# An encoder layer on one core: the second tile's scale as a dot on TensorE, in the place of products of zeros, and the square of x's last tile on VectorE

## The chip, the core and the metric

The kernel runs on one core of one Trainium2 chip. The metric is the time of the slowest core of one execution in device microseconds, here that of the only core, as the median of several runs. The core's engines are TensorE (matrix products; PE in the profile, with its weight loads as PEld), VectorE (DVE), ScalarE (ACT), GpSimd (POOL) and SyncE (SP), which here mostly issues the loads. The engines run apart from each other and wait for each other by semaphores; each works through its own row of instructions in order.

## The reference, cut to what matters

One layer of an encoder, 1024 positions of 1024 channels, in float32. A condition vector c gives six vectors of 1024 values, of which the first two scale and shift the normalised input:

```python
mod = jax.nn.silu(c) @ w_ada + b_ada
sh1, sc1, gt1, sh2, sc2, gt2 = jnp.split(mod[:, None, :], N_MOD, axis=-1)

h = rmsnorm(x, norm1_g) * (1.0 + sc1) + sh1
z = h @ w_in
u, v, q, k, va, gate_a, gate_b = jnp.split(z, cuts, axis=-1)
...
x = x + gt1 * (merged @ w_o)
h2 = rmsnorm(x, norm2_g) * (1.0 + sc2) + sh2
f_gate, f_up = jnp.split(h2 @ w_ffn_in, 2, axis=-1)
x = x + gt2 * ((jax.nn.silu(f_gate) * f_up) @ w_ffn_out)
```

`rmsnorm` divides each position by the root of the mean square of its 1024 channels. The scale of one tile of 128 channels is 128 dots of length 1024: silu(c) with 128 columns of `w_ada`.

## The kernel before, in words

The activations lie transposed: channels on the 128 partitions, positions along the row. The 1024 channels are 8 tiles (`KT`), and the positions are worked on in two halves of 512. `half(0)` opens the program. It loads x in tiles, and for each tile squares it (ScalarE or VectorE), adds two squares at a time (VectorE), and lets TensorE sum them over the partitions into `total`. From the sums come root and reciprocal (`root`, `rcol`), which TensorE spreads over the partitions into the bank `rp`.

Scale and shift of a tile are two columns of `mod`. `ada_dot` makes one column: VectorE multiplies 128 rows of `w_ada` (one output channel on each partition, 1024 weights along the row) by `silu_c`, silu(c) spread over all partitions, and accumulates along the row in one SCALAR_TENSOR_TENSOR of 128x1024; ScalarE then adds bias and gain and writes the column of `mod`. `ada_pair(k)` loads the two sets of rows for tile k: scale and shift. The sets of tiles 0 and 1 (`r`, `r1`) are loaded at the start, the first with `w_q` and `w_kv` between their halves.

Then a loop runs over the tiles k. In it VectorE makes `x = x * mod[scale] * root`, ScalarE makes the high part `hH` (a cast of x + shift to the short float32 that TensorE multiplies fast), VectorE the low part `hL`; the weights of q and k are split in the same way into `wh` (ScalarE) and `wl` (VectorE). TensorE multiplies high by high, low by high and high by low into the banks of `qps` and `kps`. In the loop's turn k the two dots for tile k+1 are made, the scale's dot ahead of `hL` of tile k and the shift's dot behind it. The halo, 128 positions of the other half, is normalised in turns 4 and 7 (`halo_four`).

While TensorE has nothing to do in the start-up it multiplies zeros into banks that will later be summed into: `open_bank` is one product of 128x512 that opens a bank, and `keep_going` adds more, in the numbers of `ZEROS = (9, 2, 7)`. The last seven stand between the spread of the root and the first real products.

All loads are issued by SyncE in the order of the program. Instructions inside `half(0)`'s start-up and loop keep the order in which the code writes them on each engine. All waits are set by the framework from the tiles that are read and written. `small`, `mid`, `wpool` and `psum` are pools with a fixed number of buffers; `at_bank` takes the next of four banks of PSUM.

The rows of `w_ada` for a scale were laid out on the host in `_layout`, as `w_ada1`: 8 pairs of 128 x 2048.

Of the kernel before, what the change touches and what calls it, by code (L numbers as in the profile page):

```python
# [8 lines left out]
F32 = mybir.dt.float32  # L9
F32R = mybir.dt.float32r  # L10
BF16 = mybir.dt.bfloat16
AF = mybir.ActivationFunctionType
ALU = mybir.AluOpType
# [3 lines left out]
P = 128  # L17
D = 1024
S = 1024
KT = D // P  # L20
# [16 lines left out]
ZEROS = (9, 2, 7)  # L37
# [4 lines left out]
def kernel(  # L42
# [43 lines left out]
    V, A, G, T = (Engine(e) for e in (nc.vector, nc.scalar, nc.gpsimd, nc.tensor))  # L86
# [3 lines left out]
    const = ctx.enter_context(pool("const"))  # L90
# [17 lines left out]
    def at_bank():  # L108
        return psum.tile([P, 512], F32, tag="at", name=nm("at"))
# [7 lines left out]
    def midt(dt, shape):  # L117
        return mid.tile([P, 2048], dt, tag="mid", name=nm("mid")).rearrange(
            "p (a b) -> p a b", a=shape
        )  # L120
# [9 lines left out]
    def load(dst, src):  # L130
        tc.keep_in_program_order(nc.sync.dma_start(dst, src))  # L131
# [40 lines left out]
    zeros = const.tile([P, P], F32R, tag="zeros", name="zeros")  # L172
    V.tensor_scalar(zeros, ones, 0.0, None, op0=ALU.mult)
    V.memset(crow, 0.0)
    identr = const.tile([P, P], F32R, tag="identr", name="identr")
# [3 lines left out]
    epsc = const.tile([P, 1], F32, tag="epsc", name="epsc")  # L179
    V.memset(epsc, EPS)  # L180

    cc = const.tile([P, 72], F32, tag="cc", name="cc")
    bada, g1c, g2c, bsT = cc[:, :48], cc[:, 48:56], cc[:, 56:64], cc[:, 64:72]
    base = const.tile([P, 48], F32, tag="base", name="base")

    def load_cond():
# [9 lines left out]
    def silu_cond(pcs, i0=0):  # L196
        for i, pc in enumerate(pcs, i0):
            A.activation(silu_c[:, i * 512 : (i + 1) * 512], pc, AF.Silu)

    mod = const.tile([P, 48], F32, tag="mod", name="mod")  # L200
    acc_mod = const.tile([P, 48], F32, tag="acc_mod", name="acc_mod")
    SH1, SC1, GT1, SH2, SC2, GT2 = (8 * i for i in range(6))
# [5 lines left out]
                                   in1=g, op0=ALU.add, op1=ALU.mult)  # L208
        V.tensor_scalar(base[:, GT1:SH2], bada[:, GT1:SH2], 0.5, None, op0=ALU.mult)

    def ada_dot(r, col, cast=None, then=None):

        c1 = slice(col, col + 1)
        V.scalar_tensor_tensor(
            out=r, in0=r, scalar=1.0, in1=silu_c, op0=ALU.mult, op1=ALU.mult,
            accum_out=acc_mod[:, c1],
        )
        if then is not None:
            then()
        if cast is not None:  # L220
            A.copy(*cast)
        factor, added = 1.0, bada
        if GT1 <= col < SH2:
            factor, added = 0.5, base
        for sc, g in ((SC1, g1c), (SC2, g2c)):
            if sc <= col < sc + 8:
                factor, added = g[:, col - sc : col - sc + 1], base
        A.activation(mod[:, c1], acc_mod[:, c1], AF.Identity, bias=added[:, c1], scale=factor)

    def ada_pair(k):  # L230
        r = midt(F32, 2)
# [59 lines left out]
    def keep_going(bank, one, zero, n):  # L291

        for _ in range(n):
            T.matmul(bank, zero, one.unsqueeze(1).to_broadcast([P, 4, P]), start=False, stop=False)
# [272 lines left out]
    def half(hf):  # L567
# [4 lines left out]
        if hf == 0:  # L572
            in_order[0] = True
            xt2 = [midt(F32, 4) for _ in range(2)]
            xt = [xt2[k // 4][:, k % 4, :] for k in range(KT)]
            halo = midt(F32, 16)
            xh, qh = halo[:, :KT, :], halo[:, KT:, :]
            hl4 = midt(F32R, 16)

            for k, n in ((0, 2), (2, 2), (4, 2), (6, 1), (7, 1)):  # L580
                load(xt2[k // 4][:, k % 4 : k % 4 + n, :].rearrange("p a b -> p (a b)"),
                     xA[:, k * HALF : (k + n) * HALF])
                if k == 2:
                    load_cond()
            hd_store = lambda q, f: f(
                hd[0, q * HALF : (q + 1) * HALF, :].rearrange("(a p) t -> p a t", p=P), xt2[q])
            load(cc, cols)
            r = ada_pair(0)
            wq0, wk0 = (wpool.tile([P, UNIT], F32, tag="raw", name=nm("raw")) for _ in range(2))
            r1 = midt(F32, 2)  # L590
            load(wq0[:, :512], w_q[0][:, :512])
            load(r1[:, 0, :], w_ada1[1, :, :D])
            load(wk0[:, :512], w_kv[0][:, :512])
            load(r1[:, 1, :], w_ada1[1, :, D:])
            load(wq0[:, 512:], w_q[0][:, 512:])
            base_bias = bias_base()
            A.activation(sm(QPK, "es"), ones[:, :QPK], AF.Silu)
            build_bias(*base_bias, range(BIAS))

            total = at_bank()  # L600
            open_bank(total, zeros, zeros)
            keep_going(total, zeros, zeros, ZEROS[0])
            cond = silu_rows()
            sqs = [midt(F32, 4) for _ in range(2)]
            sq = [sqs[k // 4][:, k % 4, :] for k in range(KT)]
            add = lambda i, j: V.tensor_tensor(sq[i], sq[i], sq[j], op=ALU.add)
            square = lambda k: A.activation(sq[k], xt[k], AF.Square)

            def square_dve(k):
                V.tensor_tensor(sq[k], xt[k], xt[k], op=ALU.mult)  # L610

            def column_sums(q, last=False):

                for i in range(NT):
                    T.matmul(total[:, i * P : (i + 1) * P], q[:, i * P : (i + 1) * P], ones,
                             start=False, stop=last and i == NT - 1)

            square(0)
            square(1)
            add(0, 1)  # L620
            column_sums(sq[0])
            square(2)
            square_dve(3)
            add(2, 3)
            column_sums(sq[2])
            square_dve(5)
            square(4)
            silu_cond(cond[:1])
            add(4, 5)
            column_sums(sq[4])  # L630
            square(6)
            square(7)
            silu_cond(cond[1:], 1)
            add(6, 7)
            column_sums(sq[6], True)
            root = sm(5, "ms")
            A.activation(root[:, :NT], total.rearrange("p (a b) -> p a b", b=P)[:, :, 0], AF.Sqrt, scale=1.0 / D, bias=epsc)
            wq, wk = ([wpool.tile([P, UNIT], F32R, tag=x, name=nm(x)) for x in ("wh", "wl")]
                      for _ in range(2))
            ada_dot(r[:, 0, :], SC1, then=ada_base)  # L640
            V.reciprocal(rcol[0][:, :NT], root[:, :NT])
            A.copy(wq[0][:, :512], wq0[:, :512])
            ada_dot(r[:, 1, :], SH1)
            rp = at_bank()
            kbk = [at_bank() for _ in range(2)]
            open_bank(kbk[0], identr, zeros)
            keep_going(kbk[0], identr, zeros, ZEROS[1])
            for i in range(NT):
                T.matmul(rp[:, i * P : (i + 1) * P], rcol[0][:, i : i + 1].to_broadcast([P, P]), ident,
                         start=True, stop=True)  # L650
            open_bank(kbk[1], identr, zeros)
            keep_going(kbk[1], identr, zeros, ZEROS[2])
            hH = [hid(), hid()]
            hL = [hid(), hid()]
        else:
            hH, hL = h_next
            in_order[0] = True
# [4 lines left out]
        if hf == 1:  # L662
            kbk = [at_bank() for _ in range(3)]
            kps = [kbk[t][:, :256] for t in range(nkv)]
        for k in range(KT):
            if hf == 0:
# [24 lines left out]
                if k == 0:  # L691
                    rb = ss_tile()[:, :HALF]
                    A.copy(rb, rp)
                    tot4 = at_bank()
                    kbk.append(at_bank())
                    kps = [kbk[t // 2][:, (t % 2) * 256 : (t % 2 + 1) * 256] for t in range(nkv)]
                elif k == 2:
                    A.activation(qh, xh, AF.Square)
                elif k == 3:
                    A.activation(root[:, NT:], tot4[:, 0:1], AF.Sqrt, scale=1.0 / D, bias=epsc)  # L700
# [31 lines left out]
                    load(xh.rearrange("p a b -> p (a b)"), xA[:, KT * HALF :])  # L732
                cast = (w_next[0], raw) if src is not None else None
                if k < KT - 1:
                    ada_dot(r[:, 0, :], SC1 + k + 1, cast)
                if k == 3:
                    V.reciprocal(rcol[0][:, NT:], root[:, NT:])
                V.scalar_tensor_tensor(out=hL[k // 4][:, k % 4, :], in0=x, scalar=sh,
# [1185 lines left out]
def _layout(inputs):  # L1924
# [10 lines left out]
    def col(v):  # L1935
        return v.reshape(-1, 128).T
# [5 lines left out]
    w_b = a["w_b"][0].reshape(2, 4, 64, 1024).transpose(1, 0, 2, 3).reshape(512, 1024)  # L1942
    w_f = a["w_ffn_in"][0]
    ada = a["w_ada"][0].T.reshape(6, 8, 128, 1024)
    out = {
        "xA": np.concatenate([xt[:, t].reshape(8, 128, -1).transpose(1, 0, 2).reshape(128, -1)
                              for t in (slice(0, 512), slice(512, 640))], axis=1),
        "xB": xt[:, 512:],
        "c": a["c"][0],
        "cols": np.concatenate([col(a["b_ada"][0]), col(a["norm1_g"][0]), col(a["norm2_g"][0]),  # L1950
                                a["gm_b_s"][0].T], axis=1),
        "rowv": np.concatenate([a["gm_v_g"][0], a["q_norm_g"][0], a["k_norm_g"][0],
                                a["attn_sink"][0]]),
        "w_ada1": ada[[1, 0]].transpose(1, 2, 0, 3).reshape(8, 128, 2048),
        "w_ada2": ada[2:].reshape(32, 128, 1024),
        "w_u": tm(w_in[:, 0:512], 2),
        "w_v": tm(w_in[:, 512:1024], 2),
# [32 lines left out]
```

## Time and profile before

| | |
|---|---|
| median of 3 runs | 1226.87 us (1226.71 to 1227.76) |
| the profiled execution | 1226.14 us, its span 1224.2 us |
| TensorE busy | 1218.0 us of the span |
| VectorE busy | 898.1 us |
| ScalarE busy | 578.9 us |
| zeros in the last group ahead of the first real product | 8 products from 13.60 us on |
| first real product | 15.59 us |

The profile is of one execution on the chip. A busy TensorE is one that has an instruction in its pipe: multiplying zeros counts as busy. Rows of the timeline merge neighbouring instructions of the same kind, so a row's duration is that of the group. In names, `mid` is any tile of the pool of that name (x, its squares, the rows of `w_ada`), `at` and `mm` are banks of PSUM, `raw` are weights as loaded, `wh` and `wl` their high and low parts. Line 79 is the helper that all compute instructions go through, line 131 the one for loads, so rows are told apart by names and shapes. The 512 KB loads of `w_ada` are 128x1024.

### The profile page before, as it was taken

To read this page: it belongs to the slowest core of one execution; us is meant where nothing else is said; L and a number is where in the kernel's file an instruction comes from. 1 tells how busy PE (TensorE), PEld (TensorE's weight loads), DVE (VectorE), ACT (ScalarE), POOL (GpSimd) and SP (SyncE) were. 2 spreads that over 40 slices of the span, in tenths; PEclk is the share of its full clock that TensorE was granted. 3 is DMA by queue.
4 is the path that set the end of the run, shared out by engine and by line. 5 is a ranking of instruction groups with operands and counts; after the bars stand their busy time and mean duration, and the time that the engine had idled before them with its cause. 6 is when DMAs were issued, how large, how long until landed. Compare 5 with 4: busy or idle time off the path is not lost.

```text
span 1224.2 us, 15615 instructions
## 1 busy us (share of the span) xinstructions
PE 1218.0 (99%) x5693; PEld 1015.8 (83%) x5693; DVE 898.1 (73%) x1450; ACT 578.9 (47%) x944; POOL 148.7 (12%) x178
## 2 busy tenths in 40 slices
PE   9999999999999999999999999999999999999998
PEld 7888888888888888888888888888888888888887
DVE  8988877788878766878797766675676766765646
ACT  5667855367855443635453233333333334433341
POOL 0024323114331000001000001010000000010001
PEclk9999999999999999999999999999999999999999
DMA  9721169621076333597413446445555439995542
GB/s 364 283 87 52 35 235 357 233 86 52 36 273 225 120 105 121 195 317 277 149 52 120 172 155 224 167 174 209 189 189 189 168 150 364 393 368 190 189 172 103
DMA packets 75936, 230.77 MB, mean 189 GB/s; under 512 B 8658, under 2 KB 8914, under 8 KB 71124
## 3 DMA queue, kind: packets, MB, share of 16 engines
q1 hardware_dynamic: 61444, 161.62, 37.4%
q0 software_dynamic: 14416, 68.17, 14.9%
q8 instruction: 44, 0.72, 0.2%
q14 instruction: 32, 0.26, 0.1%
HBM read 174.70 MB, written 55.05 MB: 188 GB/s over the span
## 4 chain that ended last, share of the span: by engine, by line
PE 98%; DMA 0%; DVE 0%; ACT 0%; issue 0%; SPq 0%; DVEq 0%; ACTq 0%
PE mm L79 51%; PE at L79 47%; DMA mid<-in_xA_dram 0%; DVE mid L79 0%; ACT mid L79 0%; ACT wh L79 0%; ACT h L79 0%; DVE crow L79 0%; ACT mod L79 0%; DVE zeros L79 0%; DVE ones L79 0%; SPq L131 0%; DVE identr L79 0%; DVEq L79 0%; ACTq L79 0%
## 5 line engine op out<-in xcount | busy, mean ns | idle before, releaser
L79 PE MATMUL mm<-mid,wh 128*128 128x512 f32 x704 | 217.4, 390 | 0.0
L79 ACT CAST wh<-raw 128x1024 fp32r<-128x1024 f32 (+1 forms) x151 | 154.4, 1024 | 118.7 <-PE mm L79 44.3
L79 DVE TENSOR_TENSOR wl<-raw,wh 128x1024 fp32r<-128x1024 f32 (+1 forms) x137 | 161.5, 1183 | 64.4 <-ACT wh L79 63.9
L79 PEld LDWEIGHTS mm<-mid,wh 128*128 128x128 f32 x704 | 131.7, 188 | 27.1
L79 PE MATMUL mm<-mid,wl 128*128 128x512 f32 x352 | 137.0, 389 | 0.0
L79 PE MATMUL mm<-wh,h 128*128 128x512 f32 x384 | 125.0, 397 | 0.2 <-ACT h L79 0.2
L79 PE MATMUL mm<-h,wh 128*128 128x512 f32 x400 | 123.9, 391 | 0.0
L79 PEld LDWEIGHTS mm<-h,wh 128*128 128x128 f32 x400 | 74.6, 188 | 15.3
L79 PE MATMUL at<-h,wh 128*128 128x512 f32 x272 | 84.0, 390 | 0.0
L79 PEld LDWEIGHTS mm<-wh,h 128*128 128x128 f32 x384 | 70.7, 188 | 14.6 <-ACT h L79 1.2
L79 DVE TENSOR_TENSOR wl<-ws,wh 128x1024 fp32r<-128x1024 f32 (+1 forms) x54 | 60.8, 1125 | 24.7 <-ACT wh L79 24.7
L79 PE MATMUL mm<-h,wl 128*128 128x512 f32 x200 | 77.9, 389 | 0.0
L79 PEld LDWEIGHTS mm<-mid,wl 128*128 128x128 f32 x352 | 66.1, 188 | 13.9
L79 ACT CAST wh<-ws 128x1024 fp32r<-128x1024 f32 (+1 forms) x54 | 52.5, 972 | 43.5 <-DVE ws L79 28.0
L79 PE MATMUL mm<-wl,h 128*128 128x512 f32 x192 | 71.2, 391 | 0.0
L79 ACT ACTIVATE t<-t 128x512 f32<-128x512 f32 x53 | 32.8, 630 | 72.8 <-DVE t L79 72.7
L79 PEld LDWEIGHTS at<-h,wh 128*128 128x128 f32 x272 | 50.9, 188 | 10.5
L79 DVE TENSOR_TENSOR ol<-raw,oh 128x1024 fp32r<-128x1024 f32 x30 | 36.6, 1224 | 30.0 <-ACT oh L79 30.0
L79 ACT ACTIVATE xs<-xs 128x512 f32<-128x512 f32 x21 | 13.3, 632 | 93.5 <-DVE xs L79 93.5
L79 PE MATMUL at<-h,wl 128*128 128x512 f32 x136 | 52.9, 389 | 0.0
L79 PE MATMUL at<-wl,wh 128*128 128x512 f32 (+1 forms) x136 | 52.7, 388 | 0.0
L79 PE MATMUL at<-wh 128*128 128x512 f32 (+1 forms) x136 | 52.7, 387 | 0.0
(271 smaller groups left out, 2731.1 us busy)
## 6 DMA issues: line engine op xcount, KB each, us to landing
raw<-in_w_gate_dram SPq DMA_DIRECT2D x28, 512.0 KB, 3.8
tA<-hid POOLq DMA_DIRECT2D x11, 1024.0 KB, 4.5
tB<-hid POOLq DMA_DIRECT2D x11, 1024.0 KB, 5.0
wo<-in_w_out_dram POOLq DMA_DIRECT2D x22, 512.0 KB, 5.8
wS<-wo POOLq DMA_DIRECT2D x11, 1024.0 KB, 5.1
raw<-wS SPq DMA_DIRECT2D x44, 256.0 KB, 3.3
raw<-tB SPq DMA_DIRECT2D x44, 256.0 KB, 4.5
mid<-in_w_ada_dram SPq DMA_DIRECT2D x20, 512.0 KB, 9.1
```

The costliest lines, as they stand in the source:

```text
L79: ins = f(*args, **kw)
```

## The change

Four things. The second tile's scale is no longer a dot on VectorE: the host lays the 128 x 1024 weights out so that eight blocks of 128x128 serve as stationary operands, and TensorE sums eight products of such a block with the silu of c's column into a slice of the bank `tot4`; ScalarE reads it there. The seven products of zeros ahead of it go. The load of those weights is issued ahead of the first half of `w_q`, and the column form of c comes with the small load `cols`, now 80 wide. The square of x's last tile is made by VectorE. The bank `tot4` is taken earlier in the code, with the same place in the pool's order.

```diff
-    cc = const.tile([P, 72], F32, tag="cc", name="cc")
+    cc = const.tile([P, 80], F32, tag="cc", name="cc")
+    ccol = cc[:, 72:80]
...
-    def ada_dot(r, col, cast=None, then=None):
+    def ada_dot(r, col, cast=None, then=None, dot=None):
         c1 = slice(col, col + 1)
-        V.scalar_tensor_tensor(
-            out=r, in0=r, scalar=1.0, in1=silu_c, op0=ALU.mult, op1=ALU.mult,
-            accum_out=acc_mod[:, c1],
-        )
+        if dot is None:
+            dot = acc_mod[:, c1]
+            V.scalar_tensor_tensor(out=r, in0=r, scalar=1.0, in1=silu_c, op0=ALU.mult, op1=ALU.mult,
+                                   accum_out=dot)
...
-        A.activation(mod[:, c1], acc_mod[:, c1], AF.Identity, bias=added[:, c1], scale=factor)
+        A.activation(mod[:, c1], dot, AF.Identity, bias=added[:, c1], scale=factor)
...
+            load(r1[:, 0, :], w_ada1[1, :, :D])
             load(wq0[:, :512], w_q[0][:, :512])
-            load(r1[:, 0, :], w_ada1[1, :, :D])
...
-            square(7)
+            square_dve(7)
             silu_cond(cond[1:], 1)
+            silu_col = sm(KT, "silu_col")
+            A.activation(silu_col, ccol, AF.Silu)
...
             open_bank(kbk[1], identr, zeros)
-            keep_going(kbk[1], identr, zeros, ZEROS[2])
+            tot4 = at_bank()
+
+            dot1 = tot4[:, 2 * P : 3 * P]
+            for i in range(KT):
+                T.matmul(dot1, r1[:, 0, i * P : (i + 1) * P], silu_col[:, i : i + 1].to_broadcast([P, P]),
+                         start=i == 0, stop=i == KT - 1)
...
-                    ada_dot(r[:, 0, :], SC1 + k + 1, cast)
+                    ada_dot(r[:, 0, :], SC1 + k + 1, cast, dot=None if k else dot1[:, :1])
...
+    ada1 = ada[[1, 0]].transpose(1, 2, 0, 3).reshape(8, 128, 2048)
+    ada1[1, :, :1024] = ada[1, 1].reshape(128, 8, 128).transpose(2, 1, 0).reshape(128, 1024)
```

Where instructions moved. First TensorE, from the column sums to the first real products (`at_221` and `at_223` are the bank `kbk[1]` before and after, `at_232` is `tot4`, `mid_139` is `r1`, `mm` are the banks of q). Before:

```order
L79 MATMUL at_157<-ones,mid_173 128x128 x8
L79 MATMUL at_220<-identr,zeros 128x512 x3
L79 MATMUL at_219<-ident,rcol_119 128x128 x4
L79 MATMUL at_221<-identr,zeros 128x512 x8
L79 MATMUL mm_241<-wh_206,h_237 128x512
```

Now:

```order
L79 MATMUL at_157<-ones,mid_173 128x128 x8
L79 MATMUL at_222<-identr,zeros 128x512 x3
L79 MATMUL at_221<-ident,rcol_119 128x128 x4
L79 MATMUL at_223<-identr,zeros 128x512
L79 MATMUL at_232<-silu_col_199,mid_139 128x128 x8
L79 MATMUL mm_245<-wh_208,h_241 128x512
```

Seven products of zeros are gone, and eight products of `r1` with the column of silu(c) stand in their place. Next VectorE in the loop's first turn (`mid_123` is x, `mid_139` is `r1`, `h_237` and `h_241` the high part, `h_239` and `h_243` the low). Before:

```order
L79 SCALAR_TENSOR_TENSOR mid_123<-mid_123,mod,at_219 128x512
L79 TENSOR_TENSOR wl_207<-raw_137,wh_206 128x512
L79 SCALAR_TENSOR_TENSOR mid_139,acc_mod<-mid_139,silu_c 128x1024
L79 SCALAR_TENSOR_TENSOR h_239<-mid_123,mod,h_237 128x512
L79 SCALAR_TENSOR_TENSOR mid_139,acc_mod<-mid_139,silu_c 128x1024
L79 SCALAR_TENSOR_TENSOR mid_123<-mid_123,mod,ss_249 128x512
```

Now:

```order
L79 SCALAR_TENSOR_TENSOR mid_123<-mid_123,mod,at_221 128x512
L79 TENSOR_TENSOR wl_209<-raw_137,wh_208 128x512
L79 SCALAR_TENSOR_TENSOR h_243<-mid_123,mod,h_241 128x512
L79 SCALAR_TENSOR_TENSOR mid_139,acc_mod<-mid_139,silu_c 128x1024
L79 SCALAR_TENSOR_TENSOR mid_123<-mid_123,mod,ss_253 128x512
```

The first of the two dots is gone, and the low part follows directly on the low part of w_q. Last SyncE's loads (`mid_134` and `mid_139` are `r` and `r1`, `raw_137` and `raw_138` the first weights of q and k). Before:

```order
L131 DMA mid_134<-in_w_ada_dram 128x1024 x2
L131 DMA raw_137<-in_w_q_dram 128x512
L131 DMA mid_139<-in_w_ada_dram 128x1024
L131 DMA raw_138<-in_w_kv_dram 128x512
L131 DMA mid_139<-in_w_ada_dram 128x1024
```

Now:

```order
L131 DMA mid_134<-in_w_ada_dram 128x1024 x2
L131 DMA mid_139<-in_w_ada_dram 128x1024
L131 DMA raw_137<-in_w_q_dram 128x512
L131 DMA raw_138<-in_w_kv_dram 128x512
L131 DMA mid_139<-in_w_ada_dram 128x1024
```

The first set of `r1` has passed the first half of `w_q`.

More of the change, by code (lines that the diff above doesn't have):

```diff
@@ L693, in half @@
                     A.copy(rb, rp)
-                    tot4 = at_bank()
                     kbk.append(at_bank())
@@ L1950, in _layout @@
         "cols": np.concatenate([col(a["b_ada"][0]), col(a["norm1_g"][0]), col(a["norm2_g"][0]),
-                                a["gm_b_s"][0].T], axis=1),
+                                a["gm_b_s"][0].T, col(a["c"][0])], axis=1),
         "rowv": np.concatenate([a["gm_v_g"][0], a["q_norm_g"][0], a["k_norm_g"][0],
                                 a["attn_sink"][0]]),
-        "w_ada1": ada[[1, 0]].transpose(1, 2, 0, 3).reshape(8, 128, 2048),
+        "w_ada1": ada1,
         "w_ada2": ada[2:].reshape(32, 128, 1024),
```

## The prediction

> **What bounds the kernel now.** First the page's totals, then the whole execution's list of waits, then busy time by stage, then the order in time of the first 40 us, in which the change lies.
>
> ```profile
> span 1224.2 us, 15615 instructions
> ...
> PE 1218.0 (99%) x5693; PEld 1015.8 (83%) x5693; DVE 898.1 (73%) x1450; ACT 578.9 (47%) x944; POOL 148.7 (12%) x178
> ```
>
> ```profile
> PE at L79 <- DVE identr L79: 1.9, 1, 1.9
> PE mm L79 <- ACT h L79: 0.2, 1, 0.2
> ```
>
> ```profile
> 14.00:16.00 2.00, 2.00 (x10) 1.41 (x9) 2.00 (x3) 1.27 (x4) 0.00 (x0) 1.00 1.04 413
> 35.00:40.00 5.00, 4.83 (x28) 3.98 (x28) 4.94 (x8) 4.27 (x10) 0.00 (x0) 1.00 1.01 411
> 400.00:800.00 400.00, 400.00 (x1780) 331.28 (x1780) 294.95 (x410) 165.01 (x235) 21.90 (x38) 1.00 0.48 168
> ```
>
> TensorE is busy for 1218.0 of 1224.2 us and in the list of waits stands for others only twice: 1.9 us at the start and 0.2 us once. From 40 us on its stream is closed (400.00 busy in 400). So the change is worth the time by which that closed stream begins earlier or later, and nothing in the rest of the kernel can add to it: its first instruction is among the first 40 us, and the instructions behind it stand in the same order as before. In these windows the third number is the span's length, PE busy follows, and the last three are granted clock, DMA share and GB/s. At 14 to 16 us TensorE seems full, but the rows below show that part of what it does there is multiplying zeros.
>
> ```profile
> 1.86 4.58 PE L79 MATMUL at<-zeros 128*128 128x512 f32 x10 [1.86 <-DVE identr L79]
> 2.03 0.20 ACT L79 ACTIVATE es<-ones 128x4 f32<-128x4 f32 x1
> ...
> 9.04 1.14 ACT L79 ACTIVATE mid<-mid 128x512 f32<-128x512 f32 x2
> ...
> 10.21 0.69 DVE L79 TENSOR_TENSOR mid<-mid 128x512 f32<-128x512 f32 x1 [0.70 <-ACT mid L79]
> ...
> 12.68 1.16 PE L79 MATMUL at<-ident,rcol 128*128 128x128 f32 x8
> ...
> 12.71 0.62 ACT L79 CAST wh<-raw 128x512 fp32r<-128x512 f32 x1
> ...
> 13.60 2.09 PE L79 MATMUL at<-identr,zeros 128*128 128x512 f32 x8
> ...
> 13.78 0.29 ACT L79 ACTIVATE mod<-acc_mod,cc 128x1 f32<-128x1 f32 x1 [0.45 <-DVE mid L79]
> 13.97 0.75 DVE L79 SCALAR_TENSOR_TENSOR mid<-mid,mod,at 128x512 f32<-128x512 f32 x1 [0.22 <-PE at L79]
> ...
> 14.81 0.73 ACT L79 ACTIVATE h<-mid,mod 128x512 fp32r<-128x512 f32 x1 [0.73 <-DVE mid L79]
> ...
> 15.23 1.22 DVE L79 SCALAR_TENSOR_TENSOR mid<-mid,silu_c 128x1024 f32<-128x1024 f32 x1
> ...
> 15.59 1.21 PE L79 MATMUL mm<-wh,h 128*128 128x512 f32 x4
> ...
> 16.38 0.75 DVE L79 SCALAR_TENSOR_TENSOR h<-mid,mod,h 128x512 fp32r<-128x512 f32 x1
> ...
> 17.04 1.22 DVE L79 SCALAR_TENSOR_TENSOR mid<-mid,silu_c 128x1024 f32<-128x1024 f32 x1
> ...
> 18.19 0.75 DVE L79 SCALAR_TENSOR_TENSOR mid<-mid,mod,ss 128x512 f32<-128x512 f32 x1
> 18.21 0.63 PE L79 MATMUL at<-wh,h 128*128 128x256 f32 x4
> ...
> 18.68 1.08 PE L79 MATMUL mm<-wl,h 128*128 128x512 f32 x4
> ...
> 19.03 0.72 ACT L79 ACTIVATE h<-mid,mod 128x512 fp32r<-128x512 f32 x1 [0.43 <-DVE mid L79]
> 19.81 0.77 PEld L79 LDWEIGHTS mm<-wh,h 128*128 128x128 f32 x4 [0.47 <-ACT h L79]
> ```
>
> The columns are start, duration of the merged group, engine, operation; x is a count, and a bracket names the idle time ahead and what ended it. Real work begins at 15.59, when ScalarE has finished the first tile of h (14.81+0.73=15.54). The second tile's products wait the same way: h at 19.03+0.72=19.75, product at 19.81. Its cause is VectorE's row of work: the dot for the second scale (15.23), the low part of h (16.38), the dot for the second shift (17.04), and only then the second tile of x (18.19). One more wait of this kind closes the start-up:
>
> ```profile
> 29.02 1.23 DVE L79 SCALAR_TENSOR_TENSOR mid<-mid,silu_c 128x1024 f32<-128x1024 f32 x1
> ...
> 33.97 0.69 DVE L79 TENSOR_TENSOR mid<-mid,at 128x512 f32<-128x512 f32 x1
> ...
> 39.89 1.20 PE L79 MATMUL mm<-wh,h 128*128 128x512 f32 x4 [0.17 <-ACT h L79]
> ```
>
> The first row is the dot for the fifth scale, the second the halo of x times its root. The third, the sixth tile's products, decides: whatever is gained at 15 or 19 us must also arrive there.
>
> **The change, part by part.** *The square of x's last tile* goes from ScalarE (1.14 for two, 0.57 each, from 9.61 on) to VectorE, which idled then (0.70 ahead of 10.21). A product of 128x512 by VectorE takes 0.69, ScalarE's took to 10.18, so the square ends near 9.57+0.69=10.26: +0.07 on the chain of column sums, root and x's first tile, which then ends at 14.79 in the place of 14.72. *The silu of the column of c* is one small instruction on ScalarE (0.20, the row of es), in the 0.57 that the square leaves; it adds nothing. If c's column came late it would hold up the root that follows at 12.15, which the freed 0.37 covers.
>
> *The zeros.* Eight products of 128x512 zeros stand at 13.60: (2.09-0.39)/7=0.24 apart, 0.39 being the last one's own duration. Seven go (1.7 us). In their place stand eight products of 128x128 in plain f32. The nearest row is the spread of the root at 12.68: 4 such products are 8 records until 13.60, 0.115 a record, so 8 products are 16 records or 1.84 us. With the one zero product that stays and the 0.07 above, TensorE is done at 13.67+0.24+1.84=15.75, against 15.52 before.
>
> *The order of loads.* The second scale's weights (512 KB) pass the first half of w_q (256 KB) in SyncE's queue.
>
> ```profile
> 5.72 0.33 SPq L131 DMA_DIRECT2D raw<-in_w_q_dram  x1
> 6.09 0.48 SPq L131 DMA_DIRECT2D mid<-in_w_ada_dram  x1
> ...
> 12.70 0.33 SPq L131 DMA_DIRECT2D raw<-in_w_kv_dram  x1
> 14.22 0.33 SPq L131 DMA_DIRECT2D mid<-in_xA_dram  x1
> ```
>
> ```profile
> raw<-in_w_q_dram SPq DMA_DIRECT2D x1, 256.0 KB, 7.0
> ```
>
> ```profile
> mid<-in_w_ada_dram SPq DMA_DIRECT2D x1, 1024.0 KB, 11.8
> ```
>
> The half of w_q landed at 5.72+7.0=12.72, just as its cast began (12.71). The 512 KB behind it take 1.3 us at the 413 GB/s of the window, so they landed near 14.0 to 14.2 (SyncE's next issue, 14.22, came with it by my reading). With the order turned round, the weights land near 13.4, before the dots want them (13.91), and the half of w_q near 14.1. The Trainium skill says the same of the mechanism: by "DMA: Bandwidth & Descriptors", section "Queues, rings and completion order", each DMA engine consumes descriptors in ring order, though completions need not be first in, first out. By it this half is later by all of the 512 KB, an estimate of 1.3 us; the trace of before has no such swap.
>
> That half is cast on ScalarE ahead of the first shift and the first h. From 14.1: cast 0.62, shift 0.29, h 0.73, less some 0.05 of overlap, so h is ready at 15.75 (before: 15.54), and the first product starts at 15.80, 0.21 late. The dots (15.75) are hidden under that. Bounds: 12.72 if the half were not delayed (then the dots set 15.75), and 14.8 if it sank behind the next half of w_kv too, with a first product at 16.5.
>
> *The second scale's dot* leaves VectorE: 17.04 minus 16.38 shows the low part costing 0.66 of its row, 18.19 minus 17.04 a dot 1.15. So 1.15 us go, but the low part now waits for h: it starts at 15.80, the shift's dot at 16.46, x's second tile at 17.61 in the place of 18.19, and h's second tile is ready near 19.17. The scale itself comes from PSUM by the same ScalarE instruction, behind the copy of the spread root, near 17.1: in time.
>
> *TensorE's first tile.* It holds 12 products of 512 columns and 8 of 256: (1.08-0.39)/3=0.23 and (0.63-0.28)/3=0.117 apart (0.28 a last one's duration), so 3.70 us, plus 0.13 for starting after a wait (1.21 against 1.08). From 15.80 it ends at 19.63, when h is there: no second wait. Before, the second tile effectively began at 19.81+0.13=19.94. Gain at this place: 0.31.
>
> *What is late next.* VectorE runs 0.58 ahead until the dot at 29.02. Its weights are the 1024 KB load, issued second of the pair of rows from 16.17 on and taking 11.8:
>
> ```profile
> 16.17 1.05 SPq L131 DMA_DIRECT2D mid<-in_w_ada_dram  x2
> ```
>
> Issued near 16.85, it lands near 28.65, because the DMA engines are full (share 1.0) and the bytes ahead are the same. So VectorE keeps at most 29.02-28.65=0.37. The halo product at 33.97 needs TensorE too, which is 0.31 ahead. Both say 0.3 to 0.4 at 39.89. Sum: +0.21 at the first product, -0.52 at the second tile (the wait for h and its start-up gone), about -0.04 more by the sixth, where VectorE's 0.37 sets the end: **-0.35**.
>
> The profiled execution is 1226.14 us (span 1224.2 and 1.9 around it), 0.73 under the median of the runs, 1226.87. So 1225.8 for a profiled execution and **1226.5** for the median.
>
> **Rivals.** (1) *Nothing is left:* the half of w_q lands near 14.5, the first product is at 16.2, and the second tile, with 3.83 behind it, begins at 20.0, level with 19.94: 1226.7 to 1227.0. For it speaks that the landing is worked out, not seen; against it the four tenths it needs at 413 GB/s would be 160 KB more ahead of it. (2) *Slower by this load:* the half lands later than 14.8, where the second x tile comes no earlier than 18.19 and the first tile's products end after 20.3; landing at 15.5 costs 0.7: 1227.6. It needs the loads to share the engines rather than follow each other. (3) *More than that:* the 1024 KB land earlier than I read, and VectorE's 0.58, or the whole 1.15 if h does not come late, reaches the sixth tile: 1225.7 to 1226.2. (4) *TensorE falls to half pace:* the zeros stand where TensorE otherwise waits, and the dots need a landing. At the start the ten zero products took (4.58-0.39)/9=0.47 each in the place of 0.24; another ten at that pace cost 2.3 us, with the idle wait before them some 3: 1230. It decides only if the weights land microseconds after 13.91; 14.2 is where they landed behind the half of w_q, so at most 0.3 of idle is in sight. The Trainium skill's "TensorE: Matmul & The Clock Gate", section "Why this matters for your kernels", puts the fall at idle gaps above about 3 us; no run here shows such a gap.
>
> **Chances.** Forecast 0.60, (1) 0.17, (2) 0.11, (3) 0.07, (4) 0.03, and 0.02 for a gain over 0.2% that I see no way to. What a measurement can tell here is 0.2%, 2.45 us; the three runs before already span 1.05. Only (4) is beyond it on the slow side, none on the fast side, and 0.01 of (2) may be: faster 0.02, same 0.94, slower 0.04. The range takes the forecast, (1), half of (2) and (3), and the runs' own spread: 1225.7 to 1227.6; the forecast's own is 1226.1 to 1226.8.
>
> **What would show it.** The cast of w_q's half starting near 14.1 after an idle time put down to a DMA; the dots from about 13.9 to 15.75, 0.115 a record; the first real product near 15.8; no wait of TensorE for h at the second tile, near 19.63; x's second tile near 17.6; the dot of the fifth scale waiting for its load near 28.7; the sixth tile at 39.5. I am wrong if the cast starts after 14.5, if the dots cost more than 0.15 a record, or if the sixth tile starts at 39.9 with everything before it earlier.

## The result: 6.3 us slower, and none of it at the place that was changed

| | before | after |
|---|---|---|
| median of 6 runs | 1226.79 us (1225.90 to 1227.76) | 1233.12 us (1232.57 to 1234.27) |
| the profiled execution | 1226.14 us, span 1224.2 | 1232.87 us, span 1231.1 |

The ratio is 1.0054 (95% interval 1.0043 to 1.0064). The forecast was 1226.5. After the change the page's totals and the list of waits say this:

```profile
span 1231.1 us, 15632 instructions
...
PE 1224.9 (100%) x5702; PEld 1016.6 (83%) x5702; DVE 897.5 (73%) x1449; ACT 578.3 (47%) x944; POOL 148.6 (12%) x178
```

```profile
PE at L79 <- DVE identr L79: 1.9, 1, 1.9
...
PE mm L79 <- ACT h L79: 0.2, 1, 0.2
```

TensorE waits for nothing new: the same two rows as before, 1.9 and 0.2 us. Yet it is busy for 6.9 us more. The start, in order of time:

```profile
13.32 0.62 ACT L79 CAST wh<-raw 128x512 fp32r<-128x512 f32 x1 [0.81 <-DMA raw<-in_w_q_dram]
...
13.74 1.95 PE L79 MATMUL at<-silu_col,mid 128*128 128x128 f32 x16
...
14.64 0.72 ACT L79 ACTIVATE h<-mid,mod 128x512 fp32r<-128x512 f32 x1 [0.50 <-DVE mid L79]
...
15.44 1.18 PE L79 MATMUL mm<-wh,h 128*128 128x512 f32 x4
...
17.21 0.75 DVE L79 SCALAR_TENSOR_TENSOR mid<-mid,mod,ss 128x512 f32<-128x512 f32 x1
...
19.23 1.07 PE L79 MATMUL mm<-wh,h 128*128 128x512 f32 x4
...
28.46 1.23 DVE L79 SCALAR_TENSOR_TENSOR mid<-mid,silu_c 128x1024 f32<-128x1024 f32 x1
...
39.20 1.20 PE L79 MATMUL mm<-wh,h 128*128 128x512 f32 x4 [0.17 <-ACT h L79]
```

The second tile's products follow without a wait at 19.23 (19.81 before), and the sixth tile's start at 39.20 (39.89 before): here the change has gained 0.69 us. The last product of each program, before and then after:

```profile
1220.05 0.28 PE L79 MATMUL mm<-wh,wl 128*128 128x256 f32 x1
```

```profile
1226.95 0.28 PE L79 MATMUL mm<-wh,wl 128*128 128x256 f32 x1
```

So from the sixth tile to the last product the same row of products took 1220.05-39.89=1180.16 us before and 1226.95-39.20=1187.75 us now: 7.59 us more. The windows show it as fewer products in the same time. Before:

```profile
40.00:400.00 360.00, 359.86 (x1852) 305.25 (x1853) 292.62 (x638) 232.74 (x482) 98.28 (x83) 1.00 0.44 157
400.00:1000.00 600.00, 600.00 (x2663) 496.86 (x2663) 433.16 (x599) 233.99 (x329) 38.94 (x70) 1.00 0.49 174
```

After:

```profile
40.00:400.00 360.00, 359.87 (x1852) 305.11 (x1851) 292.36 (x638) 232.45 (x482) 98.20 (x83) 1.00 0.46 157
400.00:1000.00 600.00, 600.00 (x2633) 491.44 (x2633) 427.02 (x591) 231.59 (x325) 38.93 (x70) 1.00 0.50 172
```

To 400 us the count is equal (1852). From 400 to 1000 us it is 2633 in the place of 2663, with PE busy for all 600.00 us and the granted clock at 1.00 in both. TensorE is slower without waiting and without a lower clock. Which products are slower is seen where two kinds follow each other. Before, then after:

```profile
719.60 0.39 PE L79 MATMUL at<-b22h,wh 128*128 128x512 f32 x1
719.83 0.39 PE L79 MATMUL at<-b22l,wh 128*128 128x512 f32 x1
720.06 0.39 PE L79 MATMUL at<-b22h,wl 128*128 128x512 f32 x1
720.28 0.39 PE L79 MATMUL at<-b22h,wh 128*128 128x512 f32 x1
```

```profile
722.13 0.40 PE L79 MATMUL at<-b22h,wh 128*128 128x512 f32 x1
722.37 0.39 PE L79 MATMUL at<-b22l,wh 128*128 128x512 f32 x1
722.59 0.40 PE L79 MATMUL at<-b22h,wl 128*128 128x512 f32 x1
722.83 0.39 PE L79 MATMUL at<-b22h,wh 128*128 128x512 f32 x1
```

Four starts span 0.68 us before and 0.70 after. From all starts in the traces: the 1008 products with a moving operand (the one that is streamed through, against the stationary one, the weights, that are loaded first and held) in `tt1`, `tt2` or `b22` start 226.9 ns apart before and 232.8 after, in turn about 229 and 238; that is 1008 x 5.9 ns = 5.95 us of the 7.59. The 48 products that hold the tiles `first` as weights went from 227.9 to 232.4 (0.2 us), and the 1056 with `mid` in `mm` from 227.4 to 228.1 (0.7 us). These last are not slower everywhere: 0.6 of the 0.7 us lies in the three products directly behind a slow group, at 40 places (231.6, 232.6 and 230.8 ns, 226.6 to 226.7 before); from the fourth on they are at 226.7 again. The rest is spread thin. The groups of the page's kind show it as the mean of one, last but one number. Before, then after:

```profile
L79 PE MATMUL mm<-mid,wh 128*128 128x512 f32 x704 | 217.4, 390 | 0.0
L79 PE MATMUL at<-tt1h,wh 128*128 128x512 f32 x112 | 43.7, 390 | 0.0
L79 PE MATMUL at<-b22h,wh 128*128 128x512 f32 x112 | 43.6, 389 | 0.0
```

```profile
L79 PE MATMUL mm<-mid,wh 128*128 128x512 f32 x704 | 217.8, 390 | 0.0
L79 PE MATMUL at<-tt1h,wh 128*128 128x512 f32 x112 | 44.2, 395 | 0.0
L79 PE MATMUL at<-b22h,wh 128*128 128x512 f32 x112 | 44.2, 394 | 0.0
```

`tt1h` and `b22h` take 395 and 394 ns, 390 and 389 before; `mid` stays at 390. Nothing in the change touches these instructions. What it does touch are the addresses in SBUF: `cc` grew from 72 to 80 columns, which moves all tiles behind it by 32 bytes in each partition, and `silu_col`, a tile of a pool with four buffers, puts 4 x 32 = 128 bytes in front of the tiles that are laid above that pool. In the built programs:

| bytes in a partition | before | after | moved |
|---|---|---|---|
| `wh` | 31936 | 31968 | 32 |
| `h` | 56512 | 56544 | 32 |
| `mid` | 89280 | 89312 | 32 |
| `b22h`, `first` | 175296 | 175456 | 160 |
| `tt1h` | 191680 | 191840 | 160 |

`b22h` lies 143360 bytes above `wh` before, 560 times 256. After it lies 128 more. `mid` and `h` moved together with `wh`. The tiles that moved against `wh` and `wl` (or, for `first`, against `h`) are those whose products are slower. `oh` and `ol`, tiles of the last part of the program, moved against `wh` and `wl` too, but are never multiplied with them; they come back below.

### The profile page after: what moved, and what is told of

Read it like the earlier page. It is cut to its first block, busy times and chain, and to the rows that moved or that the text cites. A ratio compares the mean times of both kernels' runs of the same rounds, so it can differ in the third digit from the quotient of the medians.

```text
span 1231.1 us, 15632 instructions
## 1 busy us (share of the span) xinstructions
PE 1224.9 (100%) x5702; PEld 1016.6 (83%) x5702; DVE 897.5 (73%) x1449; ACT 578.3 (47%) x944; POOL 148.6 (12%) x178
## 4 chain that ended last, share of the span: by engine, by line
PE 96%; DMA 2%; DVE 1%; ACT 0%; issue 0%; SPq 0%; DVEq 0%; ACTq 0%
PE mm L79 50%; PE at L79 46%; DMA mid<-in_w_ada_dram 1%; DMA raw<-in_w_q_dram 1%; DMA mid<-in_xA_dram 0%; DVE mid L79 0%; ACT mid L79 0%; DVE wl L79 0%; ACT wh L79 0%; SPq L131 0%; ACT h L79 0%; DVE h L79 0%; DVE crow L79 0%; ACT mod L79 0%; DVE zeros L79 0%
## 5 line engine op out<-in xcount | busy, mean ns | idle before, releaser
L79 PEld LDWEIGHTS mm<-mid,wl 128*128 128x128 f32 x352 | 66.1, 188 | 14.1
L79 PE MATMUL at<-wh,wl 128*128 128x512 f32 (+1 forms) x136 | 52.8, 388 | 0.0
```

The lines of the kernel that those rows point to most:

```text
L79: ins = f(*args, **kw)
```

## The experiments

Each kernel is timed against the kernel before on the same chip; "apart" is the mean time from start to start of the 1008 products, 226.9 ns before and 232.8 after.

### The tiles moved, with nothing else changed

**All tiles by 32 bytes**, by a wider `cc` whose end is not used:

```diff
-    cc = const.tile([P, 72], F32, tag="cc", name="cc")
+    cc = const.tile([P, 80], F32, tag="cc", name="cc")
...
-            load(cc, cols)
+            load(cc[:, :72], cols)
```

> The kernel before, with the tile of small columns 80 wide instead of 72 and the eight new columns unused: every tile behind it in SBUF lies 32 bytes higher, and the distances between the large tiles stay as they were. Theory 'distance' (TensorE streams slower when moving and stationary operand lie 128 bytes off a multiple of 512 from each other): no change, 1226.8 us, products with tt1, tt2 and b22 227 ns apart. Theory 'place' (tiles 32 bytes off a multiple of 64 are slow wherever the other operand lies): slower, some 1233. Theory 'order' (the dots, the load's new place or the earlier start bring engines or loads into each other's way later on): no change, 1226.8.

Measured: 1226.74 us, ratio 1.0005 (0.9996 to 1.0014), 226.9 ns apart. Moving everything by 32 bytes costs nothing.

**Only the upper tiles by 128 bytes**, by an unused tile at the place and in the pool of `silu_col`:

```diff
+            spare = sm(KT, "spare")
             root = sm(5, "ms")
```

> The kernel before, with one unused tile of 8 columns in the pool of small tiles (four buffers, 128 bytes): only the tiles behind that pool, among them tt1, tt2, b22 and first, lie 128 bytes higher; x, h, wh and wl stay. No instruction is added. Theory 'distance': slower by 1008 products x 6.2 ns and what trails them, 6 to 8 us, so 1233 to 1235, with products of tt1, tt2 and b22 some 233 ns apart, alternately 229 and 238. Theory 'place': no change, 1226.8, since all addresses remain multiples of 64. Theory 'order': no change, 1226.8.

Measured: 1233.12 us, ratio 1.0054 (1.0040 to 1.0068), 232.8 ns apart. In this kernel no instruction differs from before, and it has the whole loss:

```profile
400.00:1000.00 600.00, 600.00 (x2634) 491.68 (x2633) 427.00 (x591) 231.59 (x326) 38.95 (x70) 1.00 0.50 172
```

### The change, with the tiles at their old places

**The addresses of all large tiles as before:** the silu of c's column is written into columns of `acc_mod` that are not in use yet, and `epsc` moves into the end of `nhalf`, to make room for the 32 bytes of `cc`.

```diff
-            silu_col = sm(KT, "silu_col")
+            silu_col = acc_mod[:, GT2 : GT2 + KT]
...
-    V.memset(nhalf, -0.5)
-    epsc = const.tile([P, 1], F32, tag="epsc", name="epsc")
+    V.memset(nhalf[:, :15], -0.5)
+    epsc = nhalf[:, 15:16]
```

> The whole change, but without moving any large tile: the silu of the column is kept in eight columns of the accumulators that are not yet in use, and the constant epsilon shares a tile with another constant, which takes back the 32 bytes of the wider tile of columns. Theories 'distance' and 'place': the start's gain alone remains, 0.7 us at the sixth tile, so 1226.1 (ratio 0.9994). Theory 'order': as slow as the change, 1233.

Measured: 1226.08 us, ratio 0.9996 (0.9987 to 1.0005), 226.9 ns apart, the sixth tile at 39.65. The loss is gone with the change in place.

**Only the first of the two edits**, so that all tiles lie 32 bytes higher:

> The whole change, with the silu of the column in eight unused columns of the accumulators: all tiles lie 32 bytes higher, at their old distances. Theory 'distance': 1226.1, as without any move. Theory 'place': 1233. Theory 'order': 1233.

Measured: 1226.22 us, ratio 0.9996 (0.9987 to 1.0005), 226.9 ns apart, the sixth tile at 39.61. The 32 bytes of `cc` are innocent here too; the 128 of `silu_col` are the cause.

### Is it the address, or the distance between the two operands?

**All tiles by 128 bytes** (`cc` 104 columns wide, the end not used) moves the upper tiles by 128, and `wh` and `wl` with them:

> The kernel before, with the tile of small columns 128 bytes wider: all large tiles lie 128 bytes higher together, so b22 begins at 175424 as in the slow kernel with the spare tile, but wh and wl have moved with it. Theory 'distance' (what counts is the moving operand's address less the stationary one's): no change, 1226.7 us, products of tt1, tt2 and b22 226.9 ns apart. Its rival 'place by a larger modulus' (an address that is 64 or 96 modulo 256 is slow for a moving operand, wherever the weights lie): these products 232.8 ns apart, and mid, h too, since their tiles then lie at 64 modulo 256: 1233 or far more.

Measured: 1226.78 us, ratio 1.0000 (0.9990 to 1.0010), 226.9 ns apart.

```profile
L79 PE MATMUL mm<-mid,wh 128*128 128x512 f32 x704 | 217.3, 390 | 0.0
...
L79 PE MATMUL at<-tt1h,wh 128*128 128x512 f32 x112 | 43.7, 390 | 0.0
L79 PE MATMUL at<-b22h,wh 128*128 128x512 f32 x112 | 43.6, 389 | 0.0
```

The same upper tiles, moved by the same 128 bytes, are at 390 and 389 ns again: the place alone does not count, the distance to the weights does.

**The upper tiles by 32, 64 and 256 bytes**, by an unused tile of one buffer (`[P, 8]`, `[P, 16]`, `[P, 64]`):

```diff
+            spare = small.tile([P, 8], F32, tag="spare", name="spare", bufs=1)
```

> The kernel before, with one unused tile of 32 bytes in the pool of small tiles: the upper tiles lie 32 bytes off their old distance to the weights. If any distance that isn't a multiple of 512 slows the products: 232 ns or more apart and 1233 us; if the distance must reach 128: 226.9 and 1226.7.

> As before, the upper tiles 64 bytes off their old distance to the weights. If any distance that isn't a multiple of 512 slows the products: 232 ns or more apart and 1233 us; if it must reach 128: 226.9 and 1226.7.

> As before, the upper tiles 256 bytes off their old distance to the weights. If the distance counts modulo 128 or 256: 226.9 ns apart and 1226.7 us, which would leave 128 slow only for modulo 256. If it counts modulo 512 or more: 232 ns or more, 1233 us.

| upper tiles moved by | 1008 products apart | median | ratio |
|---|---|---|---|
| 0 | 226.9 ns | | 1 |
| 32 | 233.5 ns | 1236.71 us | 1.0077 (1.0056 to 1.0097) |
| 64 | 229.8 ns | 1232.57 us | 1.0043 (1.0027 to 1.0059) |
| 128 | 232.8 ns | 1233.12 us | 1.0054 (1.0040 to 1.0068) |
| 256 | 226.9 ns | 1226.58 us | 0.9997 (0.9987 to 1.0007) |

By 256 the loss is gone. The loss doesn't grow with the move: 32 bytes cost more than 128, and 64 about as much. The stretch from 400 to 1000 us, moved by 32 and by 256:

```profile
400.00:1000.00 600.00, 599.87 (x2625) 489.57 (x2624) 424.88 (x588) 231.56 (x326) 38.40 (x69) 1.00 0.49 171
```

```profile
400.00:1000.00 600.00, 599.92 (x2662) 496.66 (x2661) 432.70 (x598) 233.39 (x329) 38.93 (x70) 1.00 0.50 173
```

2625 products against 2662. With 32 and 64 the products with `mid` in `mm` slow down as well, to 228.7 and 229.2 ns on the mean (227.4 before), though `mid` did not move against the weights. The traces show where: only directly behind the slow groups, in the first 7 products at 32 bytes and in the first 10 at 64, against 3 at 128; the ones behind these are at 226.3 to 226.9 ns again. So a slow group has a tail. At 64 bytes the tail adds 2.0 us to the 2.9 us that the 1008 products lose, at 128 bytes only 0.6 to 5.9, which is most of why the two cost about as much in all.

**The weights moved instead:** an unused tile of 128 bytes ahead of `wh` and `wl`, and a second behind them, so that these two move by 128 and all tiles behind them by 256. Then `mid`, `h` and the upper tiles all lie 128 bytes off.

```diff
+    wpool.tile([P, 32], F32, tag="spare0", name="spare0", bufs=1)
...
+            wpool.tile([P, 32], F32, tag="spare1", name="spare1", bufs=1)
```

> The kernel before, with one unused tile of 128 bytes ahead of wh and wl and one behind them: the weights lie 128 bytes higher, every tile behind them 256 bytes, so only the distance between the weights and everything else has changed (modulo 256). Theory 'distance to the weights': now all products of wh or wl with mid, h, tt1, tt2 and b22, some 3900 of 512 columns, are 6 ns slower: 233 ns apart and 1247 to 1253 us. Rival 'distance to what VectorE and ScalarE read and write meanwhile': these distances are the old ones modulo 256, apart from wh and wl themselves: 227 ns, 1226.8 us.

Measured: 1247.32 us, ratio 1.0161 (1.0145 to 1.0178), 20.5 us more than before.

```profile
L79 PE MATMUL mm<-mid,wh 128*128 128x512 f32 x704 | 221.3, 395 | 0.0
...
L79 PE MATMUL mm<-h,wh 128*128 128x512 f32 x400 | 126.0, 396 | 0.0
...
L79 PE MATMUL at<-b22h,wh 128*128 128x512 f32 x112 | 44.3, 396 | 0.0
L79 PE MATMUL at<-tt1h,wh 128*128 128x512 f32 x112 | 44.3, 396 | 0.0
...
L79 PE MATMUL at<-wl,wh 128*128 128x512 f32 x134 | 52.2, 389 | 0.0
```

Now `mid` and `h` are slow too (395 and 396 ns). Two groups are the counter-check: products of `wl` with `wh`, which moved together, stay at 389, and `first` with `h`, which both moved by 256, are back at 226.9 ns apart, although `first` was slow after the change. So the pace goes with the distance, modulo 256 bytes, between the tile that is streamed and the weights.

Whose weights, the product's own or those of the next one, these runs hardly part: in the 1008 products both lie off alike. The traces show that the load of the next product's weights runs during a product (it begins 2 to 4 ns after it and takes 187 to 188). In the last part of the program groups of products with `wh` and `wl` take turns with groups of `oh` and `ol`, each with both operands of its own kind. At the 30 changes from one kind to the other a product's own two operands lie a multiple of 256 apart in every kernel here, and only the next product's weights can lie off. One such place, before and then after:

```profile
1018.58 0.39 PE L79 MATMUL at<-wh,wl 128*128 128x512 f32 x1
1018.80 0.39 PE L79 MATMUL at<-oh 128*128 128x512 f32 x1
```

```profile
1025.17 0.40 PE L79 MATMUL at<-wh,wl 128*128 128x512 f32 x1
1025.40 0.39 PE L79 MATMUL at<-oh 128*128 128x512 f32 x1
```

All 30 take 227 ns to the next start before and 232 after; the mean is 232.3 with the weights moved, 235.0 with the upper tiles moved by 32 bytes and 226.8 by 256, but 225.8 by 64. So at 128 and at 32 bytes the weights that are loaded meanwhile are enough. Whether the distance to a product's own weights costs anything of itself is not shown: the only products that have it alone stand beside or behind slow ones.

### What the change is worth without the loss

**`silu_col` as 8 of 16 columns of its tile**, so that its four buffers take 256 bytes in the place of 128:

```diff
-            silu_col = sm(KT, "silu_col")
+            silu_col = sm(2 * KT, "silu_col")[:, :KT]
```

> The change with one number altered: the tile of the column's silu is 16 columns wide in the place of 8, so its four buffers take 256 bytes and the upper tiles are 256 bytes off their old distance. Theory 'distance modulo 256': products of tt1, tt2 and b22 227 ns apart, 1226.2 us, as in the version with the old places. If anything else of the change made the later products slow: 1233.

Measured: 1226.02 us, ratio 0.9995 (0.9986 to 1.0004), 226.8 ns apart. The two other steps were then undone in this version, one at a time: the order of the two loads, and the last square, back on ScalarE.

> The change with the silu tile of 16 columns, and the first half of w_q loaded ahead of the second scale's weights, as in the kernel before. The prediction's working: the half's cast no longer waits for a load, but the weights land near 14.1, so the dots start some 0.3 us late and end near 15.9; the first product is at 15.9 in the place of 15.8 and the sixth tile within 0.2 us: 1226.1. Rival, that the order of these loads carries the start's gain: the second tile's products wait for h again, and the sixth tile is where it was before (39.9 on the mean of the looks): 1226.8.

Measured: 1226.24 us, ratio 0.9997 (0.9988 to 1.0006). With the old order the cast of `w_q`'s half waits for nothing, and the dots wait for their weights instead:

```profile
12.44 0.61 ACT L79 CAST wh<-raw 128x512 fp32r<-128x512 f32 x1
...
14.24 2.02 PE L79 MATMUL at<-silu_col,mid 128*128 128x128 f32 x16 [0.33 <-DMA mid<-in_w_ada_dram]
```

> The change with the silu tile of 16 columns, and the square of x's last tile on ScalarE again. The prediction's working: the square on VectorE costs 0.07 us of the chain and the one on ScalarE nothing here, as the root waits for the sums: 1226.0 to 1226.2, the sixth tile within 0.1 us beside the jitter of x's landing. Rival, that the square on VectorE brings the gain: the column sums end later than with it, and 1226.8.

Measured: 1226.21 us, ratio 0.9995 (0.9985 to 1.0005). The two medians differ from 1226.02 by 0.2 us, less than the intervals: neither step is told apart from no change. The five kernels with the change, or most of it, and without the loss lie at 0.9995 to 0.9997, 0.4 to 0.8 us under the kernel before, and every interval holds 1: all point to a small gain, none shows it.

## Why the prediction was wrong, and where it held

**The step that failed** is in its first part: "nothing in the rest of the kernel can add to it: its first instruction is among the first 40 us, and the instructions behind it stand in the same order as before". The order did stay, and no wait came in. But the step took the pace of a closed stream as given, and the pace changed: 7.59 us behind the sixth tile, of which the kernel with nothing but the unused tile shows 7.45 (1180.16 us from the sixth tile to the last product before, 1187.61 there, 1187.75 after). The second half of the same error is in the costing: the silu of the column "adds nothing" was true of its 0.20 us of ScalarE, but its tile was not costed, and neither was the wider `cc`. The four rivals were all events of the start; none let the rest of the kernel become slower, so the slower side had 0.04.

**The start**, step by step, in the profiles of after, of the old places, of all by 32 and of the 256-byte tile:

| step | said | measured |
|---|---|---|
| cast of `w_q`'s half, waiting for its load | 14.1 | 13.32, 14.39, 14.16, 14.57 |
| dots of the second scale | 16 records of 0.115 | 16, 0.112 from start to start in all four |
| first real product | 15.80 | 15.44, 16.01, 15.79, 16.19 |
| x's second tile on VectorE | 17.61 | 17.21, 17.80, 17.58, 17.99 |
| second tile's products, with no wait for h | 19.63 | 19.23, 19.85, 19.60, 20.04 |
| fifth scale's dot, said to be held by its load | 28.65 | 28.46, 28.65, 28.88, 28.87 |
| sixth tile's products | 39.5 | 39.20, 39.65, 39.61, 39.84 |

The chain was right in its order. What makes the four differ is mostly when the half of `w_q` lands: in three of them the first product follows the start of the cast by 1.62 or 1.63 us, and in the first, where the cast started at 13.32, h waits 0.50 us for x on VectorE instead. (The prediction's own sum of this step, 14.1+0.62+0.29+0.73-0.05, is 15.69 and not 15.75; it changes nothing of the account.) The arrival of x differs from one execution to the next as well: over all profiles the wait for a late load of x ends between 7.25 and 8.39 us. The fifth scale's dot started 0.02 to 0.03 us behind the landing of its load in three of the four; in the second the load was there 0.14 us earlier. The mechanism of the load held: the half of `w_q` behind 512 KB is what the cast waits for (0.81 to 1.82 us), in the 256-byte version at 14.57:

```profile
14.57 0.62 ACT L79 CAST wh<-raw 128x512 fp32r<-128x512 f32 x1 [1.50 <-DMA raw<-in_w_q_dram]
```

That agrees with the ring order of the Trainium skill's "DMA: Bandwidth & Descriptors", section "Queues, rings and completion order". The size of the gain cannot be read from two profiles: 39.89 to 39.20 is 0.69, but the seven profiles whose start is that of before (without the one with the moved weights, where the start's products are slower too) have the sixth tile between 39.33 and 40.33, mean 39.89, and the four above have a mean of 39.58. The difference, -0.31, looks like the -0.35 of the sum, but two of the seven (the upper tiles by 32 and by 64 bytes) had another start: TensorE's four products with c followed each other at up to 0.85 us in the place of 0.50 at most, and the column sums began at 8.74 and 8.84 in the place of 7.60 to 7.99. Without these two the mean is 39.73 and the difference -0.15, in values that spread by 0.85. So the sum is neither borne out nor refuted; the medians without the loss (-0.4 to -0.8 us) do not speak against it.

**The rivals:** the half of `w_q` landing late (1, 2) was seen in part (14.57 in one execution, the second tile at 20.04) and came to no loss that could be measured; TensorE at half pace (4) did not occur: no idle time stands ahead of the dots in any of the four, and their records start 0.112 us apart, against the 0.115 of the forecast.

## What to carry to other kernels

A small new tile is an edit to every tile behind it. Before costing a change at its own place, compare the addresses of the streamed tiles and of the weights of the large products in the two built programs, and keep their distance in steps of 256 bytes by rounding the new tile up (here 16 columns in the place of 8 took the whole 7 us away). When a program is slower and no engine waits longer, compare the number of products in the same stretch of time and the mean of one product by group: a mean that goes from 390 to 395 ns in some groups only, with the clock at 1.00, points to the operands and not to the schedule.

## What the runs showed of the hardware

- The 1008 products of 128x512 in the short float32 started 226.9 ns apart where the streamed tile and the weights lay a multiple of 256 bytes apart in the partition, and 229.8 to 233.5 ns apart where they lay 32, 64 or 128 bytes off that; the whole program's time hung on such distances by 0.4 to 1.6% (1.6% with the weights moved, where `mid` and `h` lay off too).
- At the 30 places where only the next product's weights, loaded meanwhile, lay 128 bytes off, the product took 232 ns in the place of 227.
- After the change the slower products start in turn 229 and 238 ns apart, so it is not an equal price on each, and the slow pace lasts 3 products (128 bytes off), 7 (32) or 10 (64) beyond the group that causes it.
- It does not come from VectorE or ScalarE: after the change, those of the 1008 that fell into a time when both were idle were 233.4 ns apart (116 of them, 226.7 before), and those with both busy for over half of it 233.3 (133 of them, 226.9 before).

Open is the mechanism. Whether the weight load or the stream is held up, why every other product pays more, why the tail is longer at 32 and 64 bytes, why at 64 the 30 places cost nothing, and what other distances than these do, is not shown.
